# FFN up product with the tokens stationary, its output turned by 32x32 VectorE transposes and a trip through DRAM

## The chip, the core and the metric

One core of a Trainium2 chip runs the whole program: TensorE (PE; its weight loads are shown apart as PEld), VectorE (DVE), ScalarE (ACT), GpSimd (POOL, hardly used here) and SyncE (SP, which issues every DMA of this kernel). The metric is the device time of one execution in microseconds (us).

## What is computed

A decoder trunk of two layers over 256 tokens with 2048 features, in float32. Each layer has a mixer, a cross-attention into 256 memory tokens and a gated feed-forward part (FFN) with a short convolution over the tokens. The change concerns the FFN alone:

```python
def conv_ffn(h, w_up, conv_w, conv_b, w_down):     # h 256 x 2048, w_up 2048 x 11264
    u = causal_dwconv(h @ w_up, conv_w) + conv_b   # 3 taps over tokens, per feature
    g, val = jnp.split(u, 2, axis=-1)
    return (jax.nn.silu(g) * val) @ w_down         # w_down 5632 x 2048
```

`h` is normalised first; the factor of each token (one over its root mean square) is multiplied in after `h @ w_up`, before the convolution.

## The kernel before

Activations lie with features on the 128 partitions and the 256 tokens along the free axis. To keep precision, each operand is split in two float32r parts, high and low, and a product is three partial products: high·high, high·low, low·high. An activation operand `x` has, for each 128 features, 512 columns: 256 tokens high, then 256 low.

`stream` brings in weights: SP loads 1024 columns (512 KB, a **weight tile** in what follows) into `raw` (4 buffers), ACT casts them to `wh`, DVE subtracts to get `wl` (3 buffers of each). Two products use it:

- `wstat` keeps weights stationary. For each 128 input features (a k step; there are 16) and each 128 output features it loads `wh` and streams all 512 columns of `x`, then loads `wl` and streams the 256 high columns. The result has features on partitions, with high and low halves side by side; `fold` adds the halves (ACT copies one out, DVE adds).
- `xstat` keeps tokens stationary. For each k step and each 128 tokens it does three matmuls, each of which streams 512 weight columns: `xh` with `wh`, `xh` with `wl`, `xl` with `wh`. The result has tokens on partitions and 512 features along the free axis. The value projections (`vp`) and the queries of the windowed attention (`zq`) use it.

The FFN up product (`ffn_up`) runs 44 calls of `wstat` per layer, each of 256 features: 128 gate features and the 128 values that they multiply. `ffn_tile` follows each: `fold`, `by_row` (the token factors `rbc`, on DVE), the three taps (one ACT activation with bias, two DVE multiply-adds over shifted tokens, for each of the two halves), Silu on ACT, the product, and `split` into the high and low parts of the operand `a` of the down product.

Engines run their instructions in order. A scheduler at build time sets that order; casts, subtractions and the first reads of a result have priority. Functions that the change touches, with the lines of the profile:

Of the kernel before, what the change touches and what calls it, by code (L numbers as in the profile page):

```python
# [9 lines left out]
F32 = mybir.dt.float32  # L10
# [4 lines left out]
ALU = mybir.AluOpType  # L15
AX = mybir.AxisListType

P = 128
# [5 lines left out]
FT = D_FF // P  # L24
# [22 lines left out]
WPRIO = 100  # L47
# [17 lines left out]
class Task:  # L65


    def __init__(self, gen, after):
        self.gen, self.after, self.wait, self.done = gen, after, 0, False


class Trunk:
    def __init__(self, ctx, tc, a):
        self.tc, self.nc, self.a = tc, tc.nc, a
        pool = lambda name, bufs, **kw: ctx.enter_context(tc.tile_pool(name=name, bufs=bufs, **kw))
        self.const = pool("const", 1)
        self.par = pool("par", 1)
        self.actp = pool("actp", 29)
        self.raw = pool("raw", 4)
        self.wp = pool("wp", 3)  # L80
        self.tmp = pool("tmp", 6)
        self.ev = pool("ev", 3)
        self.col = pool("col", 3)
        self.rb = pool("rb", 2)
        self.pmm = pool("pmm", 2, space=bass.MemoryType.PSUM)
        self.psm = pool("psm", 4, space=bass.MemoryType.PSUM)

        self.tasks = deque()
# [105 lines left out]
    def xstat_both(self, xs, wd, name="mm"):  # L194

        nc = self.nc
        ps = [self.pmm.tile([P, 2, 512], F32, tag="mm", name=name)]
        side = [self.bank(name) for _ in range(2)]
        out = [[ps[0][:, tb, :TOKC] for tb in range(2)], [b[:, :TOKC] for b in side]]
        for k, wh, wl in self.stream(wd, 2 * TOKC, KT):  # L200
            x = xs(k // 2) if callable(xs) else xs[k // 2]
            for tb in range(2):
                xh, xl = (x[:, k % 2, u, tb * P:(tb + 1) * P] for u in range(2))
                for lhs, w, i in ((xh, wh, 0), (xh, wl, 1), (xl, wh, 2)):
                    for c in range(2):
                        nc.tensor.matmul(out[c][tb], lhsT=lhs, rhs=w[:, c * TOKC:(c + 1) * TOKC],  # L206
                                         start=(k == 0 and i == 0), stop=(k == KT - 1 and i == 2))
                self.pump()
        return out


    def fold(self, ps, name="z", z=None):
# [685 lines left out]
        return out, ts  # L898


    def ffn_tile(self, ps, j, rbc, x):
        nc = self.nc
        z = self.fold(ps)
        self.by_row(z, rbc)
        u = self.t512("u", (P, 2, T))
        for s in range(2):
            m = 2 * j + s
            tap = [self.p[:, C_FW + m * 3 + i:C_FW + m * 3 + i + 1] for i in range(3)]
            nc.scalar.activation(u[:, s, :], z[:, s, :], AF.Identity, bias=self.p[:, C_FB + m:C_FB + m + 1], scale=tap[2])  # L909
            nc.vector.scalar_tensor_tensor(u[:, s, 1:T], z[:, s, 0:T - 1], tap[1], u[:, s, 1:T], ALU.mult, ALU.add)  # L910
            nc.vector.scalar_tensor_tensor(u[:, s, 2:T], z[:, s, 0:T - 2], tap[0], u[:, s, 2:T], ALU.mult, ALU.add)
        nc.scalar.activation(u[:, 0, :], u[:, 0, :], AF.Silu)
        nc.vector.tensor_tensor(u[:, 1, :], u[:, 0, :], u[:, 1, :], ALU.mult)
        self.split(x[:, j % 2, 0, :], x[:, j % 2, 1, :], u[:, 1, :])

    def ffn_up(self, l, xs, acc):
        out, wait = [], []
        _, rbc, rt = self.row_factor(acc, "rx", W["ss"])
        for j in range(FT):
            wait.append((self.wstat(xs, self.a["wu"][l, j], name="up"), j))  # L920
            if j == 0:
                continue
            self.until(rt)
            for ps, i in wait:
                if i % 2 == 0:
                    out.append(self.operand(f"a{i // 2}"))
                self.ffn_tile(ps, i, rbc, out[-1])
            wait = []
        return out

    def run(self):
# [23 lines left out]
def _groups(w, gc):  # L955

    d, k, n = w.shape
    w = w.reshape(d, k // P, P, n // gc, gc).transpose(0, 3, 2, 1, 4)
    return np.ascontiguousarray(w).reshape(d, n // gc, P, (k // P) * gc)


def _fm(x):

    return np.ascontiguousarray(x.T.reshape(8, 2, P, T).transpose(0, 2, 1, 3))


def _colmajor(v):

    return np.swapaxes(v.reshape(v.shape[:-1] + (-1, P)), -1, -2)


def _layout(inp):
    sizes = (256, 256, 512, 512, 16, 1024, 128, 128, 512, 512, 512)
    off = np.concatenate([[0], np.cumsum(sizes)])
    gq, gk, gv, gr, lr, sq, sk, sv, cb, cc, ch = (np.arange(off[i], off[i + 1]) for i in range(11))
    heads = sq.reshape(2, 8, 64).transpose(1, 0, 2).reshape(-1)
    fm = [gk, gq, gr]
    for j in range(4):
        fm += [cc[j * P:(j + 1) * P], ch[j * P:(j + 1) * P]]
    w_in = inp["w_in"]  # L980
    d = {}
    d["w_tok"] = _groups(w_in[:, :, np.concatenate([lr, sk, sv, gv])], 2 * TOKC)[:, 0]
    d["w_fm"] = _groups(w_in[:, :, np.concatenate(fm + [cb])], 2 * P)
    d["w_q"] = _groups(w_in[:, :, heads], 512)
    ro = np.arange(2048)
    rows = np.concatenate([ro[1536:], ro[:512],
                           512 + np.arange(1024).reshape(2, 8, 64).transpose(1, 0, 2).reshape(-1)])
    d["wo"] = _groups(inp["w_out"][:, rows, :], 256)
    for n, m in (("wq", "xa_wq"), ("wk", "xa_wk"), ("wxo", "xa_wo"), ("wd", "ffn_w_down")):
        d[n] = _groups(inp[m], 256)  # L990
    d["wd7"] = _groups(inp["ffn_w_down"][-1:, :, 14 * P:], P)[0]
    d["wv"] = _groups(inp["xa_wv"], 512)
    pair = np.arange(2 * D_FF).reshape(2, FT, P).transpose(1, 0, 2).reshape(-1)
    d["wu"] = _groups(inp["ffn_w_up"][:, :, pair], 256)
    d["x"], d["mem"] = _fm(inp["x"][0]), _fm(inp["mem"][0])
    d["mem"] = d["mem"].reshape(4, 2, P, 2, T).transpose(0, 2, 1, 3, 4)
    d["xt"] = inp["x"][0].reshape(2, P, D)
    d["memt"] = inp["mem"][0].reshape(2, P, D)
    d["gmix0"] = _colmajor(inp["norm_mix"][0])
    d["pos"] = inp["positions"].reshape(2, P).T  # L1000
    d["wgate"] = inp["gla_w_gate"]
    d["sinks"] = inp["swa_sinks"]
    d["gfin"] = _colmajor(inp["norm_final"])
    par = np.zeros((DEPTH, P, NPAR), np.float32)
    for c, n in ((C_MIX, "norm_mix"), (C_X, "norm_x"), (C_MEM, "norm_mem"), (C_FFN, "norm_ffn")):
        par[:, :, c:c + 16] = _colmajor(inp[n])
    par[:, :, C_GB:C_GB + 2] = _colmajor(inp["gla_b_gate"])
    par[:, :, C_GN] = inp["gla_norm"]
    par[:, :, C_SC:C_SC + 12] = _colmajor(inp["sc_conv"]).transpose(0, 2, 3, 1).reshape(DEPTH, P, 12)
    fc = inp["ffn_conv"][:, :, pair]  # L1010
    par[:, :, C_FW:C_FW + 264] = _colmajor(fc).transpose(0, 2, 3, 1).reshape(DEPTH, P, 264)
    par[:, :, C_FB:C_FB + 88] = _colmajor(inp["ffn_conv_b"][:, pair])
    d["par"] = par
    con = np.zeros((P, NCON), np.float32)
    con[:, Q_ID:Q_ID + P] = np.eye(P)
    rel = np.arange(P)[:, None] + P - np.arange(T)[None, :]
    con[:, Q_MASK:Q_MASK + T] = np.where((rel >= 0) & (rel < P), 0.0, -1e30)
    con[:, Q_INV:Q_INV + 32] = np.array(ROPE_INV, np.float32)
    d["con"] = con
    s, t = np.arange(P)[:, None] % 64, np.arange(64)  # L1020
    lev = []
    for n in LEVELS:
        tn = t[t % n >= n // 2][None, :]
        lev.append((s // n == tn // n) & (s % n < n // 2))
    lev.append(s == t[None, :])
    d["lev"] = np.concatenate(lev, axis=1).astype(np.int32)
    return {n: np.ascontiguousarray(v) for n, v in d.items()}
# [18 lines left out]
```

## Time and profile before

| | |
|---|---|
| time, median of 3 runs | 2925.98 us (2925.84 to 2926.13) |
| the profiled execution | 2925.97 us, of it 2923.8 us span on the core |
| PE, PEld busy | 2903.3 us (99%), 2524.3 us (86%) |
| DVE, ACT busy | 1926.9 us (66%), 1506.3 us (52%) |
| DMA | 532.41 MB, mean 182 GB/s |
| granted TensorE clock | 1.00 in the FFN up stages |

A matmul's shown duration runs from its entry to its modelled end and overlaps the next one's; the distance between the starts of neighbours tells what one costs. DMAs show the time from issue to landing.

### The profile page before, as it was taken

How to read it: one execution, taken by the hardware profiler on the slowest of the kernel's cores; microseconds unless marked ns; L12 is line 12 of the kernel's file. 1: busy time of each engine (PE TensorE's matmuls, PEld its weight loads, DVE VectorE, ACT ScalarE, POOL GpSimd, SP SyncE). 2: the span in 40 equal slices, each digit the busy share in tenths (PEclk: the TensorE clock that was granted, in tenths of full speed). 3: DMA queues.
4: the chain of work that ended last, by engine and by line, in shares of the span. 5: the costliest groups of instructions: out<-in, count | busy, mean ns of one | idle time of the engine just before them, and what ended most of it. 6: DMA issues, size and time to landing. Idle time of an engine off the chain costs nothing.

```text
span 2923.8 us, 42872 instructions
## 1 busy us (share of the span) xinstructions
PE 2903.3 (99%) x16718; PEld 2524.3 (86%) x16718; DVE 1926.9 (66%) x2867; ACT 1506.3 (52%) x2125; POOL 8.0 (0%) x38
## 2 busy tenths in 40 slices
PE   9999999999999999999999999999999999999998
PEld 8888888888888888888888888888888888888887
DVE  6786665556777777655567766655577777776454
ACT  6565444444555555544455654444455555554443
POOL 0000000000000000000000000000000000000000
PEclk9999999999999999999999999999999999999999
DMA  7556655555565656666664566555556565656664
GB/s 241 157 179 200 189 184 166 173 168 185 185 188 184 190 183 189 190 188 188 183 183 139 168 194 188 185 163 169 173 183 188 184 188 186 188 187 188 188 188 144
DMA packets 149164, 532.41 MB, mean 182 GB/s; under 512 B 17216, under 2 KB 17760, under 8 KB 148960
## 3 DMA queue, kind: packets, MB, share of 16 engines
q1 hardware_dynamic: 148960, 529.66, 59.0%
q8 instruction: 131, 2.15, 0.3%
q14 instruction: 73, 0.60, 0.1%
HBM read 527.50 MB, written 2.10 MB: 181 GB/s over the span
## 4 chain that ended last, share of the span: by engine, by line
PE 98%; DVE 1%; ACT 0%; DMA 0%; issue 0%; SPq 0%; DVEq 0%
PE up L171 21%; PE res L171 19%; PE up L172 11%; PE res L172 9%; PE kp L171 4%; PE qp L171 4%; PE vp L189 2%; PE vp L190 2%; PE vp L188 2%; PE kp L172 2%; PE qp L172 2%; PE tokp L206 2%; PE zc L171 2%; PE up L175 1%; PE zq L190 1%; PE zq L188 1%
## 5 line engine op out<-in xcount | busy, mean ns | idle before, releaser
L156 DVE TENSOR_TENSOR wl<-raw,wh 128x1024 fp32r<-128x1024 f32 (+2 forms) x993 | 1204.2, 1213 | 721.1 <-ACT wh L155 719.2
L155 ACT CAST wh<-raw 128x1024 fp32r<-128x1024 f32 (+2 forms) x993 | 1033.2, 1041 | 939.5 <-PE res L171 303.2
L171 PE MATMUL up<-xs,wh 128*128 128x512 f32 x2640 | 935.9, 399 | 0.0
L172 PE MATMUL up<-xs,wl 128*128 128x256 f32 x2640 | 742.3, 281 | 0.0
L171 PEld LDWEIGHTS up<-xs,wh 128*128 128x128 f32 x2640 | 496.4, 188 | 117.8
L172 PEld LDWEIGHTS up<-xs,wl 128*128 128x128 f32 x2640 | 499.6, 189 | 3.5
L171 PE MATMUL res<-a,wh 128*128 128x512 f32 x1376 | 482.6, 395 | 0.0
L172 PE MATMUL res<-a,wl 128*128 128x256 f32 x1376 | 386.1, 281 | 0.0
L171 PEld LDWEIGHTS res<-a,wh 128*128 128x128 f32 x1376 | 258.1, 188 | 59.8
L172 PEld LDWEIGHTS res<-a,wl 128*128 128x128 f32 x1376 | 260.5, 189 | 0.8
L171 PE MATMUL qp<-xs,wh 128*128 128x512 f32 x480 | 171.2, 397 | 0.0
L171 PE MATMUL res<-xo,wh 128*128 128x512 f32 x480 | 170.5, 399 | 0.0
L171 PE MATMUL kp<-ms,wh 128*128 128x512 f32 x480 | 169.5, 397 | 0.0
L172 PE MATMUL res<-xo,wl 128*128 128x256 f32 x480 | 134.9, 281 | 0.0
L172 PE MATMUL qp<-xs,wl 128*128 128x256 f32 x480 | 134.9, 281 | 0.0
L219 ACT COPY z_b<-up 128x512 f32<-128x512 f32 x88 | 51.6, 587 | 161.3 <-PE up L175 161.3
L172 PE MATMUL kp<-ms,wl 128*128 128x256 f32 x480 | 134.7, 281 | 0.0
L220 DVE TENSOR_TENSOR z<-up,z_b 128x512 f32<-128x512 f32 x88 | 60.8, 691 | 105.7 <-ACT z_b L219 105.7
L909 ACT ACTIVATE u<-z,par 128x256 f32<-128x256 f32 x176 | 96.6, 595 | 48.5 <-DVE z L224 48.5
L171 PEld LDWEIGHTS res<-xo,wh 128*128 128x128 f32 x480 | 90.3, 188 | 21.2
L171 PEld LDWEIGHTS kp<-ms,wh 128*128 128x128 f32 x480 | 90.2, 188 | 21.1
L171 PEld LDWEIGHTS qp<-xs,wh 128*128 128x128 f32 x480 | 90.2, 188 | 18.8
(317 smaller groups left out, 4078.4 us busy)
## 6 DMA issues: line engine op xcount, KB each, us to landing
raw<-in_wu SPq DMA_DIRECT2D x352, 512.0 KB, 4.4
raw<-in_wd SPq DMA_DIRECT2D x175, 512.0 KB, 3.6
raw<-in_w_fm SPq DMA_DIRECT2D x80, 512.0 KB, 4.4
raw<-in_wk SPq DMA_DIRECT2D x64, 512.0 KB, 4.8
raw<-in_wo SPq DMA_DIRECT2D x64, 512.0 KB, 4.5
raw<-in_wq SPq DMA_DIRECT2D x64, 512.0 KB, 3.9
raw<-in_wv SPq DMA_DIRECT2D x64, 512.0 KB, 3.7
raw<-in_wxo SPq DMA_DIRECT2D x64, 512.0 KB, 4.3
```

The source lines that it names most:

```text
L155: nc.scalar.copy(wh[:, :n], raw[:, :n])
L156: nc.vector.tensor_tensor(wl[:, :n], raw[:, :n], wh.bitcast(F32)[:, :n], ALU.subtract)
L171: nc.tensor.matmul(ps[:, m, :], lhsT=wh[:, ms], rhs=xhl, start=(k == 0), stop=False)
L172: nc.tensor.matmul(ps[:, m, 0:T], lhsT=wl[:, ms], rhs=xh, start=False, stop=False)
L175: nc.tensor.matmul(ps[:, m, :], lhsT=wh[:, ms], rhs=xhl, start=False, stop=True)
L188: nc.tensor.matmul(ps[:, tb, :gc], lhsT=xh, rhs=wh, start=(k == 0), stop=False)
L189: nc.tensor.matmul(ps[:, tb, :gc], lhsT=xh, rhs=wl, start=False, stop=False)
L190: nc.tensor.matmul(ps[:, tb, :gc], lhsT=xl, rhs=wh, start=False, stop=(k == KT - 1))
L206: nc.tensor.matmul(out[c][tb], lhsT=lhs, rhs=w[:, c * TOKC:(c + 1) * TOKC], start=(k == 0 and i == 0), stop=(k == KT - 1 and i == 2))
L219: nc.scalar.copy(b, ps[:, :, T:2 * T])
L220: nc.vector.tensor_tensor(z, ps[:, :, 0:T], b, ALU.add)
L909: nc.scalar.activation(u[:, s, :], z[:, s, :], AF.Identity, bias=self.p[:, C_FB + m:C_FB + m + 1], scale=tap[2])
```

## The change

The up product goes through `xstat`: 22 calls per layer, each of 512 features (two gate/value pairs), with the weights laid out by the host in groups of 512 columns. The result has tokens on partitions and must be turned. `turn` does this in two steps. Two DVE transposes (one for each 128 tokens) read PSUM and turn every 32x32 block within its own 32 partitions, into `zt` (`z_t` in the rows). Then a DMA writes `zt` (512 KB) to a DRAM tile `zd` (`z_d`), and four DMAs read it back, each for 32 partitions, into `zf` (shown as `z`), so that the blocks come to the right partitions. Two DVE multiplications put in the token factors, in place of `by_row`, and write the result over `zt`. `fold` is gone here. The taps and what follows are as before. A constructor argument of the program (`dynamic_dma_scratch_size=1024`) gives back memory for the new buffers.

```diff
+        self.turnp = pool("turnp", 2)
+        self.dram = pool("dram", 4, space=bass.MemoryType.DRAM)
...
+    def turn(self, ps, name="z"):
+        nc = self.nc
+        zt = self.turnp.tile([P, 4, 2, 4, 32], F32, tag="zt", name=name + "_t")
+        zf = self.turnp.tile([P, 4, 2, 4, 32], F32, tag="zf", name=name)
+        zd = self.dram.tile([4, 32, 4, 256], F32, tag="zd", name=name + "_d")
+        with self.tc.high_priority(offset=WPRIO):
+            for tb in range(2):
+                nc.vector.transpose(out=zt[:, :, tb].rearrange("p b k i -> p k b i"),
+                                    in_=ps[:, tb, :].rearrange("p (k b i) -> p k b i", k=4, b=4))
+            nc.sync.dma_start(zd.rearrange("a p b f -> (a p) (b f)"), zt.rearrange("p b t k i -> p (b t k i)"))
+            for b in range(4):
+                nc.sync.dma_start(zf[32 * b:32 * b + 32].rearrange("p a t k i -> p a (t k i)"),
+                                  zd[:, :, b, :].rearrange("a p f -> p a f"))
+        return zf, zt.rearrange("p b t k i -> p (b t k i)").rearrange("p (k t) -> p k t", k=4)
...
-    def ffn_tile(self, ps, j, rbc, x):
-        z = self.fold(ps)
-        self.by_row(z, rbc)
+    def ffn_tile(self, z, j, x):
...
     def ffn_up(self, l, xs, acc):
...
-        for j in range(FT):
-            wait.append((self.wstat(xs, self.a["wu"][l, j], name="up"), j))
+        for j in range(0, FT, 2):
+            zf, z = self.turn(self.xstat(xs, self.a["wu"][l, j // 2], name="up"))
...
+            for tb in range(2):
+                ts = slice(tb * P, (tb + 1) * P)
+                nc.vector.tensor_tensor(z[:, :, ts].rearrange("p k (a i) -> p k a i", a=4),
+                                        zf[:, :, tb].rearrange("p a k i -> p k a i"),
+                                        rbc[:, ts].rearrange("p (a i) -> p a i", a=4).unsqueeze(1)
+                                        .broadcast_to([P, 4, 4, 32]), ALU.mult)
+            out.append(self.operand(f"a{j // 2}"))
+            for i in range(2):
+                self.ffn_tile(z[:, 2 * i:2 * i + 2], j + i, out[-1])
...
-    d["wu"] = _groups(inp["ffn_w_up"][:, :, pair], 256)
+    d["wu"] = _groups(inp["ffn_w_up"][:, :, pair], 512)
```

On SP, at the start of an FFN up stage, the kernel before issues nothing but weight loads (176 of `wu` for the layer):

```order
L153 DMA raw<-in_wxo 128x1024 x32
L153 DMA raw<-in_wu 128x1024 x176
L153 DMA raw<-in_wd 128x1024 x6
```

The changed kernel issues there, for each block of 512 features (8 weight tiles), one write and four reads more:

```order
L155 DMA raw<-in_wxo 128x1024 x32
L155 DMA raw<-in_wu 128x1024 x14
L225 DMA z_d<-z_t 128x1024
L155 DMA raw<-in_wu 128x1024
L227 DMA z<-z_d 32x4x256 x4
L155 DMA raw<-in_wu 128x1024 x7
```

The first block's write stands behind 14 weight loads: the 8 of its own block and tiles 0 to 5 of the next one. Its reads stand behind tile 6.

On DVE, in the middle of the stage, the kernel before has these rows from one `wl` to the next `fold` (a half of 512 features):

```order
L156 TENSOR_TENSOR wl<-raw,wh 128x1024
L220 TENSOR_TENSOR z<-up,z_b 128x512
L224 TENSOR_TENSOR z<-z,rxb 128x512
L156 TENSOR_TENSOR wl<-raw,wh 128x1024
L910 SCALAR_TENSOR_TENSOR u<-z,par,u 128x255 x2
L911 SCALAR_TENSOR_TENSOR u<-z,par,u 128x254 x2
...
L913 TENSOR_TENSOR u<-u 128x256
...
L228 TENSOR_TENSOR a_7249<-u,a_7249 128x256
```

The changed kernel has these rows on DVE for a whole block, from the transposes of a block (when PE has ended it) on; between rows that are left out with "..." there is one `wl` row each time:

```order
L223 STREAM_TRANSPOSE z_t<-up 128x4x4x32 x2
L158 TENSOR_TENSOR wl<-raw,wh 128x1024 x3
L944 TENSOR_TENSOR z_t<-z,rxb 128x4x128 x2
L158 TENSOR_TENSOR wl<-raw,wh 128x1024
L928 SCALAR_TENSOR_TENSOR u<-z_t,par,u 128x255 x3
L929 SCALAR_TENSOR_TENSOR u<-z_t,par,u 128x254
L928 SCALAR_TENSOR_TENSOR u<-z_t,par,u 128x255
L929 SCALAR_TENSOR_TENSOR u<-z_t,par,u 128x254 x2
L158 TENSOR_TENSOR wl<-raw,wh 128x1024
L929 SCALAR_TENSOR_TENSOR u<-z_t,par,u 128x254
L931 TENSOR_TENSOR u<-u 128x256
...
```

The `wl` of tiles 0 and 1 of the next block stand ahead of the transposes, those of tiles 2, 3 and 4 between them and the multiplications (L944), which wait for the four reads; tile 5 follows, then seven of the eight tap instructions, then tile 6.

## Rows read from the trace of the kernel before

**Rows 1.** Busy time by engine, and the chain that ended last, shares by engine.

```profile
PE 2903.3 (99%) x16718; PEld 2524.3 (86%) x16718; DVE 1926.9 (66%) x2867; ACT 1506.3 (52%) x2125; POOL 8.0 (0%) x38
...
PE 98%; DVE 1%; ACT 0%; DMA 0%; issue 0%; SPq 0%; DVEq 0%
```

**Rows 2.** The first FFN up stage: us, busy time (instructions), granted clock, DMA share, GB/s.

```profile
715.60:1213.50 497.90, 497.90 (x2826) 432.63 (x2825) 368.60 (x538) 281.80 (x396) 0.00 (x0) 1.00 0.60 186
```

**Rows 3.** Matmuls with `wh` of that stage (as many with `wl`): count, ns minimum/median/maximum, first and last start.

```profile
L171 PE MATMUL up<-xs,wh x1320: 386/398/479, 715.6 to 1212.4; 128*128 128x512 f32 x189
...
L175 PE MATMUL up<-xs,wh x88: 391/394/401, 726.7 to 1213.2; 128*128 128x512 f32 x88
```

**Rows 4.** Its first matmul and the one after its last: start, us, instruction.

```profile
715.62 0.39 PE L171 MATMUL up<-xs,wh 128*128 128x512 f32 x1
...
1213.46 0.39 PE L171 MATMUL res<-a,wh 128*128 128x512 f32 x1
```

**Rows 5.** Value projection by `xstat`: the ends of an uninterrupted run of 30.

```profile
535.18 0.39 PE L189 MATMUL vp<-wl,ms 128*128 128x512 f32 x1
...
541.98 0.39 PE L189 MATMUL vp<-wl,ms 128*128 128x512 f32 x1
```

**Rows 6.** Queries by `xstat`: the ends of a run of 14 behind other matmuls.

```profile
1560.78 0.40 PE L188 MATMUL zq<-wh,xs 128*128 128x512 f32 x1
...
1564.01 0.39 PE L190 MATMUL zq<-wh,xs 128*128 128x512 f32 x1
```

**Rows 7.** DVE and ACT, 800 to 1200 us: count, busy us, mean ns, idle before.

```profile
L156 DVE TENSOR_TENSOR wl<-raw,wh 128x1024 fp32r<-128x1024 f32 x142 | 173.4, 1221 | 58.3 <-ACT wh L155 58.3
L155 ACT CAST wh<-raw 128x1024 fp32r<-128x1024 f32 x142 | 148.6, 1047 | 76.8 <-PE up L171 76.8
...
L220 DVE TENSOR_TENSOR z<-up,z_b 128x512 f32<-128x512 f32 x35 | 24.2, 692 | 44.1 <-ACT z_b L219 44.1
L224 DVE TENSOR_TENSOR z<-z,rxb 128x512 f32<-128x512 f32 x35 | 24.2, 691 | 1.2
L219 ACT COPY z_b<-up 128x512 f32<-128x512 f32 x35 | 20.5, 587 | 66.4 <-PE up L175 66.4
```

**Rows 8.** DVE in order of time, in the first up stage.

```profile
808.82 1.22 DVE L156 TENSOR_TENSOR wl<-raw,wh 128x1024 fp32r<-128x1024 f32 x1
809.95 0.87 DVE L910 SCALAR_TENSOR_TENSOR u<-z,par,u 128x255 f32<-128x255 f32 x2
810.74 0.87 DVE L911 SCALAR_TENSOR_TENSOR u<-z,par,u 128x254 f32<-128x254 f32 x2
...
812.66 0.42 DVE L913 TENSOR_TENSOR u<-u 128x256 f32<-128x256 f32 x1
...
819.51 0.69 DVE L224 TENSOR_TENSOR z<-z,rxb 128x512 f32<-128x512 f32 x1
820.12 1.22 DVE L156 TENSOR_TENSOR wl<-raw,wh 128x1024 fp32r<-128x1024 f32 x1
```

**Rows 9.** DMA issues 801 to 860 us, and the first output write: count, size, issue to landing.

```profile
raw<-in_wu SPq DMA_DIRECT2D x22, 512.0 KB, 4.5
...
out<-h SPq DMA_DIRECT2D x1, 256.0 KB, 2.1
```

**Rows 10.** A DMA issued at 1213.43 us between weight loads, and the very first DMA.

```profile
lr<-in_wgate SPq DMA_DIRECT2D x1, 16.0 KB, 4.3
...
gmix<-in_gmix SPq DMA_DIRECT2D x1, 8.0 KB, 1.6
```

**Rows 11.** Weight loads of the down product, two sizes, whole span.

```profile
raw<-in_wd SPq DMA_DIRECT2D x175, 512.0 KB, 3.6
...
raw<-in_wd SPq DMA_DIRECT2D x2, 256.0 KB, 2.7
```

**Rows 12.** SP's issues at the start: start, us, DMA.

```profile
0.74 0.39 SPq L315 DMA_DIRECT2D gmix<-in_gmix  x1
1.19 0.42 SPq L153 DMA_DIRECT2D raw<-in_w_tok  x1
```

More of the change, by code (lines that the diff above doesn't have):

```diff
@@ L916, in ffn_up @@
     def ffn_up(self, l, xs, acc):
-        out, wait = [], []
+        nc = self.nc
+        out = []
         _, rbc, rt = self.row_factor(acc, "rx", W["ss"])
-        for j in range(FT):
-            wait.append((self.wstat(xs, self.a["wu"][l, j], name="up"), j))
+        for j in range(0, FT, 2):
+            zf, z = self.turn(self.xstat(xs, self.a["wu"][l, j // 2], name="up"))
             if j == 0:
[L922 to L928, printed above, removed]
+                self.until(rt)
+            for tb in range(2):
[7 more added lines that the diff above has]
+                self.ffn_tile(z[:, 2 * i:2 * i + 2], j + i, out[-1])
         return out
@@ L1034 @@
     arrays = _layout({n: np.asarray(v) for n, v in inputs.items()})
-    nc = bacc.Bacc("TRN2", target_bir_lowering=False, num_devices=1)
+    nc = bacc.Bacc("TRN2", target_bir_lowering=False, num_devices=1, dynamic_dma_scratch_size=1024)
     feeds, aps = {}, {}
```

## The prediction

> **What bounds the kernel now.** I read the page's busy shares and chain first, then the stretch of the stage that changes. PE is busy 99% of the span and 98% of the chain [rows 1]; in the FFN up stage it has no idle time at all (497.90 of 497.90 us at granted clock 1.00), while DVE is busy 74%, ACT 57% and the DMA engines 60% [rows 2]. So the stage lasts as long as PE's stream of matmuls, and only two things can move the time: what that stream costs, and whether anything makes PE wait for weights.
>
> What one matmul costs is not its shown duration, since neighbours overlap, but the distance between starts. The first stage has 1320 + 88 matmuls with `wh` and as many with `wl`, so 1408 pairs [rows 3], and lasts from 715.62 to 1213.46 us [rows 4]: 497.84 / 1408 = 353.6 ns a pair of 512 + 256 columns. The second layer's stage is alike.
>
> **The matmuls.** For one k step and 512 features the old form needs 4 pairs, 4 x 353.6 = 1414 ns. The new one needs 6 matmuls of 512 columns (two token blocks by three partial products). The trace has that form already, in the value projection: 30 distances in a row take 541.98 - 535.18 = 6.80 us, 226.7 ns each [rows 5]. 6 x 226.7 = 1360 ns. The columns streamed are equal (4 x 768 = 6 x 512 = 3072); what goes is a quarter of the instructions and of the weight loads. The saving is 54.3 ns a unit; there are 16 k steps x 22 blocks x 2 layers = 704 units: **-38.2 us**. Behind an interruption the same form runs for a while at (1564.01 - 1560.78) / 14 = 230.7 ns [rows 6]; were all of the stage like that, 1384 ns a unit and -21 us. The up stage has next to no other matmuls to interrupt it, so I take 226.7.
>
> At this place the Trainium skill speaks against the change: "TensorE: Matmul & The Clock Gate", section Back-to-back issue gap, puts an isolated matmul of N columns at N / 2.4 + 2.5 ns, so time follows columns. By it a pair costs 325 ns, a unit 1300 before and 1295 after, and the saving is an estimated 4 us. The trace does not agree: 353.6 ns against 325, and 226.7 against 215.8.
>
> **The turn, and who waits for it.** A block now takes 96 x 226.7 ns = 21.76 us of PE, a weight tile an eighth, 2.72 us. Per block of 512 features, `fold`'s two DVE additions (0.692) and two `by_row` (0.691) go [rows 7]; two transposes and two multiplications come. All read or write the same 512 columns, the transposes from PSUM as the addition did. No row shows a transpose. Below, 0.61 us, the pace of one instruction of that size to the next (820.12 - 819.51) [rows 8]; above, twice 0.69 if a block is filled and drained without overlap, 1.4. I take 0.69, because it moves as many elements in and out as the addition. ACT loses its two copies of 0.587 [rows 7]. Two instructions of one kind pass in 0.79 us (810.74 - 809.95), a `wl` in 1.13 (809.95 - 808.82) [rows 8]. DVE's work per block is then 8 x 1.13 + 2 x 0.65 + 2 x 0.65 + 8 x 0.395 + 4 x 0.42 = 16.5 us of 21.76. DVE has enough time; what counts is its order.
>
> DVE works in order, and the multiplications wait for the round trip through DRAM at the head of its queue. Behind them stand the `wl` that PE needs next. Let the block end on PE at 0. Transposes until 1.4 us. SP has then passed tile 5's load and stands at the write. A write of 256 KB lands after 2.1 us [rows 9]; a load of 512 KB takes 0.9 us longer than one of 256 [rows 11], so 3.0 us alone, and at most the 4.5 us of weight loads in this stream [rows 9], since a tile's load is under way ahead of it. I take 4.0: landed at 5.4. The four reads are issued 0.45 us apart (1.19 - 0.74) [rows 12], the last 1.4 us after the first. Its landing takes 1.6 us on an empty queue, 4.3 among weight loads [rows 10]; tile 6's load, issued at about 2.6, is nearly through by then, so I take 2.4. The data are there at Z = 1.4 + 4.0 + 1.4 + 2.4 = **9.2 us**; the bounds are 1.4 + 3.0 + 1.4 + 1.6 = 7.4 and 1.4 + 4.5 + 1.4 + 4.3 = 11.6.
>
> Which of the `wl` behind is late first? From Z on: two multiplications 1.3, tile 5's `wl` 1.13, seven tap instructions 2.75, tile 6's `wl` 1.22: done at Z + 6.4. PE begins tile 6 at 6 x 2.72 = 16.3 and its second matmul, the first that needs `wl`, at 16.55. So DVE may wait until **Z = 10.15** before PE stops; tile 5 (needed at 13.8, done at Z + 2.4) would bear more. At Z = 9.2 the wait of DVE is hidden, with 0.95 us to spare. Each microsecond beyond 10.15 comes back once in a block, 44 times: PE stops, the next block ends later, and so on.
>
> ACT's casts are further from their limit: tile 6's cast (1.047, [rows 7]) stands behind four activations that follow the multiplications, and ends near Z + 4.5, ahead of DVE.
>
> SP's own queue: behind the write waits tile 6's load, behind the reads tile 7's. The latter is issued at 5.4 + 1.8 = 7.2 instead of about 5.1 (when tile 3's `wl` frees its buffer), lands within 4.5 us at 11.7, and PE wants the tile at 19.0: hidden by 7 us. The DMA engines carry 8 x 512 KB plus twice 512 KB per 21.76 us, so 241 GB/s in place of 186; by the same cost per byte that is 60% x 241 / 186 = 78% of them. The reads move 1 KB pieces and may cost more; there is room for it. At the end of each stage the last block's turn runs beside the down product, whose PE needs that operand last in its first sweep over 44 k steps, some 30 us later at 2 pairs a step.
>
> Sum, against the profiled execution's 2925.97 us (which is the median of 2925.98): -38.2, and nothing for the turn: **2888 us**.
>
> **Rivals.**
>
> *The round trip is late (slower).* The mechanism is the one above with Z past 10.15: multiplications hold DVE, tile 6's `wl` comes late, PE stops once in every block. It cancels the saving at 10.15 + 38.2 / 44 = 11.0 us, and decides from there. At the upper bound, Z = 11.6, it costs 1.45 x 44 = 64 us: 2926 - 38 + 64 = 2952. Transposes of 1.4 us alone put Z at 10.6: +20, 2908; together with the upper bound Z = 13.0 and 3013. For it speaks that two dependent DMAs stand in a row and share the engines with the weights; against it, that the nearest write takes 2.1 us, half of what I allow. Chance of ending slower 0.25; of a partial loss that still leaves it faster, 0.12.
>
> The Trainium skill's "DMA: Bandwidth & Descriptors", section Anatomy of one DMA — SWDGE (gpsimd) path, says that the receipt of a write is slowest into HBM. Here the trace has an HBM write of 256 KB at 2.1 us beside loads of that size at 2.7.
>
> *Columns alone set PE's time.* If a unit costs what its 3072 columns cost in the old form (353.6 / 768 = 0.460 ns a column), 1414 ns stay 1414 and the time is 2926. Against it: 226.7 / 512 = 0.443 ns a column in rows of this trace, in a stage with the same casts and subtractions beside it. Chance 0.06. (The formula of the Trainium skill's page "TensorE: Matmul & The Clock Gate", section Back-to-back issue gap, would come out here, 4 us below 2926.)
>
> *The slower spacing*, 230.7 ns all along, as queues behind DVE's transposes or PSUM reads might make it: 2905. Chance 0.10, within "faster".
>
> **Numbers.** The likeliest case, all of the gain, has 0.47, partial loss 0.12, slower spacing 0.10: faster 0.69. Columns alone 0.06, which with a wait that just cancels the gain makes "within 0.2%" 0.06; slower 0.25. A measurement of this kernel can tell about 0.2% (6 us) from no change. The likeliest case's own range is 2884 to 2894: 4 us below for a spacing 1 ns shorter than any row shows, 6 above for short stops. The range that holds 8 in 10 reaches down to 2884 and up to the round trip's upper bound, 2952; slower transposes together with a slow round trip are left out.
>
> **What would show it.** The matmuls `up<-wh,xs` at 226 to 228 ns from start to start, 2112 in a stage, and stages of 479 us. PE without idle time in them. The transposes near 0.7 us. DVE waiting for the four reads at L944 for 1 to 2 us a block, with the reads landing 8 to 10 us after the block's last matmul. If I am wrong, PE's idle time stands ahead of tile 6 in each block, released by `wl`, and the reads' landing or the transposes say which; or the spacing is over 230 ns with PE never idle.

## The result and the profile after

The changed kernel takes 2948.58 us (2948.32 to 2948.97, 4 runs) against 2926.06 us beside it: ratio 1.0077, 95% interval 1.0063 to 1.0091, so 22.5 us slower where 38 us faster had been forecast. What came true is the rival of the late round trip, which the prediction had given 0.25.

The page after, with busy time by engine and the shares of the chain that ended last [rows 1]:

```profile
PE 2884.8 (98%) x15310; PEld 2445.7 (83%) x15310; DVE 1914.7 (65%) x2867; ACT 1460.6 (50%) x2037; POOL 8.0 (0%) x38
...
PE 73%; DMA 12%; DVE 10%; issue 3%; SPq 2%; ACT 0%; DVEq 0%
```

TensorE's share of the chain falls from 98 to 73%, and the transfers of the turn stand in it. Both FFN up stages, in windows from their first matmul to their last (us, then busy time by engine, granted clock, DMA share, GB/s) [rows 2]:

```profile
715.00:1223.10 508.10, 489.09 (x2121) 394.80 (x2121) 359.29 (x530) 257.59 (x349) 0.00 (x0) 1.00 0.70 225
2174.20:2683.70 509.50, 489.11 (x2123) 394.89 (x2122) 359.35 (x530) 257.60 (x349) 0.00 (x0) 1.00 0.70 224
```

A stage lasts 508 to 510 us instead of 498, and TensorE, which had no idle time there, now shows 19 to 20 us of it in each (less than the stops cost, as shown below); the two stages account for 10.2 + 11.6 = 21.8 of the 22.3 us by which the span grew. The tile `up` tells what the matmuls, the transposes and the waits for them are (ns minimum/median/maximum; idle time in us, times) [rows 3]:

```profile
L190 PE MATMUL up<-wh,xs x1408: 387/389/476, 715.0 to 2683.0; 128*128 128x512 f32 x176
...
L191 PE MATMUL up<-wl,xs x1408: 387/389/504, 715.3 to 2683.2; 128*128 128x512 f32 x176
...
L223 DVE STREAM_TRANSPOSE z_t<-up x88: 673/696/718, 738.0 to 2684.5; 128x512 f32<-128x512 f32 x88
...
  DVE wl L158: 104.3, 117
```

The transposes are as priced, 0.696 us. It is `wl` that TensorE waits for, and the waits of the whole span say why (who waits for whom: us in all, times, longest):

```profile
DVE z_t L944 <- DMA z<-z_d: 150.7, 44, 5.0
...
PEld up L191 <- DVE wl L158: 64.9, 63, 1.9
```

By the starts of the matmuls, TensorE stops ahead of tile 6's second matmul in 41 of the 42 blocks that follow another one in their stage (0.7 to 1.3 us from start to start), and in 15 of them ahead of tile 5's as well (0.39 to 1.86 us). VectorE stands at the multiplications (L944) in every one of the 44 blocks, 3.4 us on average, where 1 to 2 us had been forecast. The chain that ended last, in order of time, through one block of the first stage (start, us, what):

```profile
805.39 0.24 PE up L192
805.70 0.60 issue
806.30 0.69 DVE z_t L223
807.00 4.70 DMA z_d<-z_t
811.72 0.33 SPq L227
812.04 0.06 issue
812.10 0.75 SPq L227
812.89 0.43 SPq L227
813.36 3.92 DMA z<-z_d
817.41 0.10 DVE z_t L944
817.50 0.51 issue
818.02 0.68 DVE z_t L944
818.70 1.14 DVE wl L158
819.84 1.19 DVE u L928 x3
...
822.52 1.23 DVE wl L158
823.79 0.50 PE up L191
```

This is the first rival link by link: the block's last matmul, transposes, write (4.70 us), four issues, the last read (3.92 us), then behind the multiplications tile 5's `wl`, taps, tile 6's `wl`, and only then TensorE's matmul with tile 6's `wl` at 823.79. This trip, 11.8 us, is so long that TensorE stops for tile 5's `wl` too, which ends at 819.84. Its timeline there (idle time before an instruction in brackets):

```profile
819.06 0.39 PE L190 MATMUL up<-wh,xs 128*128 128x512 f32 x1
819.89 0.50 PE L191 MATMUL up<-wl,xs 128*128 128x512 f32 x1 [0.45 <-DVE wl L158]
820.23 0.39 PE L192 MATMUL up<-wh,xs 128*128 128x512 f32 x1
```

0.83 us pass between the first two starts where 0.227 would do. The bracket says 0.45 because the first matmul's shown duration runs on; distances between starts are again the measure. (The prediction let tile 5 bear a trip of 13.8 - 2.4 = 11.4 us; this one is longer.)

### The profile page after: what moved, and what is told of

Read it like the earlier page. It is cut to its first block, busy times and chain, and to the rows that moved or that the text cites. A ratio compares the mean times of both kernels' runs of the same rounds, so it can differ in the third digit from the quotient of the medians.

```text
span 2946.1 us, 40277 instructions
## 1 busy us (share of the span) xinstructions
PE 2884.8 (98%) x15310; PEld 2445.7 (83%) x15310; DVE 1914.7 (65%) x2867; ACT 1460.6 (50%) x2037; POOL 8.0 (0%) x38
## 4 chain that ended last, share of the span: by engine, by line
PE 73%; DMA 12%; DVE 10%; issue 3%; SPq 2%; ACT 0%; DVEq 0%
PE res L173 18%; PE res L174 9%; DMA z_d<-z_t 7%; DMA z<-z_d 5%; PE kp L173 4%; PE qp L173 4%; PE up L191 4%; DVE wl L158 4%; PE up L192 3%; PE up L190 3%; DVE u L928 2%; PE vp L192 2%; PE vp L190 2%; PE vp L191 2%; PE qp L174 2%
## 5 line engine op out<-in xcount | busy, mean ns | idle before, releaser
L191 PE MATMUL up<-wl,xs 128*128 128x512 f32 x1408 | 555.4, 394 | 39.4 <-DVE wl L158 39.4
L192 PE MATMUL up<-wh,xs 128*128 128x512 f32 x1408 | 548.9, 390 | 0.0
L190 PE MATMUL up<-wh,xs 128*128 128x512 f32 x1408 | 548.5, 390 | 0.0
L191 PEld LDWEIGHTS up<-wl,xs 128*128 128x128 f32 x1408 | 264.1, 188 | 118.7 <-DVE wl L158 64.9
L190 PEld LDWEIGHTS up<-wh,xs 128*128 128x128 f32 x1408 | 264.3, 188 | 55.8
L192 PEld LDWEIGHTS up<-wh,xs 128*128 128x128 f32 x1408 | 264.4, 188 | 53.0
L927 ACT ACTIVATE u<-z_t,par 128x256 f32<-128x256 f32 x176 | 91.6, 591 | 144.7 <-DVE z_t L944 144.7
L944 DVE TENSOR_TENSOR z_t<-z,rxb 128x512 f32<-128x512 f32 x88 | 56.9, 689 | 150.7 <-DMA z<-z_d 150.7
```

The source lines that it names most:

```text
L190: nc.tensor.matmul(ps[:, tb, :gc], lhsT=xh, rhs=wh, start=(k == 0), stop=False)
L191: nc.tensor.matmul(ps[:, tb, :gc], lhsT=xh, rhs=wl, start=False, stop=False)
L192: nc.tensor.matmul(ps[:, tb, :gc], lhsT=xl, rhs=wh, start=False, stop=(k == KT - 1))
L944: nc.vector.tensor_tensor(z[:, :, ts].rearrange("p k (a i) -> p k a i", a=4), zf[:, :, tb].rearrange("p a k i -> p k a i"), rbc[:, ts].rea ...
```

## The experiments

**First round: is it the order on VectorE, the traffic, or the matmuls?** Theory A: the round trip's end holds VectorE at the head of its queue, and with it the `wl` behind. Theory B: the traffic, or SyncE standing still for the write, holds up the weight loads. Theory C: the matmul form or the transposes cost more than thought.

*late6* holds back the multiplications and what follows them on VectorE until a later `wl` has been issued; no data, buffer or DMA changes:

```diff
-            zf, z = self.turn(self.xstat(xs, self.a["wu"][l, j // 2], name="up"))
...
+            first = len(self.wls)              # wls: every wl subtraction, in order
+            ps = self.xstat(xs, self.a["wu"][l, j // 2], name="up")
+            if held:
+                with self.tc.issue_after(self.wls[first + 6].ins):
+                    finish(*held)              # multiplications and ffn_tile of the block before
+            held = (*self.turn(ps), j)
```

> Only the order on VectorE changes: the two multiplications of a block, which wait for the four reads, stand behind the subtraction (wl) of tile 6 of the next block instead of tile 4; all DMAs stay. Theory A (the trip's end, 11.1 us after the block, holds VectorE at the head of its queue and so delays the wl of tile 6): tile 6's wl is no longer behind the wait, TensorE does not stop, stages of 479 to 481 us, 2888 to 2893 us. Theory B (the trip's traffic, and SyncE's queue that stands still for the write, hold up the weight loads themselves): about 2948 us as before, with casts waiting for loads.

Measured: 2892.24 us (ratio 0.9885, 0.9871 to 0.9900), within A's numbers.

*lateT* goes further: the multiplications of a block are issued behind the transposes of the next one.

```diff
+            zf, z, turned = self.turn(ps)      # turned: the second transpose
+            if held:
+                with self.tc.issue_after(turned.ins):
+                    finish(*held)
```

> The multiplications of a block are issued on VectorE only behind the transposes of the next block, a whole block (21.8 us) later, so no trip of 11 to 13 us can hold VectorE; all DMAs stay. Theory A: VectorE never waits for the reads, 2888 to 2895 us. Theory B: about 2948 us.

Measured: 2889.61 us (0.9877, 0.9860 to 0.9893), 59 us below the changed kernel and 36.5 below the kernel before, the fastest version that leaves nothing out. Its stages (windows as above) have no idle time on TensorE, though the DMA engines carry the same turn at a higher rate. They are 28 to 30 us shorter than the changed kernel's, and that is what the stops cost there:

```profile
714.90:1194.60 479.70, 479.70 (x2121) 397.42 (x2120) 355.66 (x516) 254.36 (x341) 0.00 (x0) 1.00 0.76 239
2145.10:2624.90 479.80, 479.80 (x2123) 397.46 (x2122) 355.76 (x516) 254.32 (x341) 0.00 (x0) 1.00 0.76 239
```

and VectorE passes from transposes to multiplications without a wait, since what they need landed 12 us earlier (the write of this turn was issued at 804.49, and its trip of 11.1 us ended at 814.04):

```profile
824.91 1.31 DVE L224 STREAM_TRANSPOSE z_t<-up 128x512 f32<-128x512 f32 x2 [0.41 <-PE up L193]
826.15 1.25 DVE L942 TENSOR_TENSOR z_t<-z,rxb 128x512 f32<-128x512 f32 x2
827.32 1.22 DVE L159 TENSOR_TENSOR wl<-raw,wh 128x1024 fp32r<-128x1024 f32 x1
```

*notrip* leaves out the write and the reads; the transposes write `zf` and the multiplications read it:

```diff
-            nc.sync.dma_start(zd.rearrange("a p b f -> (a p) (b f)"), zt.rearrange("p b t k i -> p (b t k i)"))
-            for b in range(4):
-                nc.sync.dma_start(zf[32 * b:32 * b + 32].rearrange("p a t k i -> p a (t k i)"),
-                                  zd[:, :, b, :].rearrange("a p f -> p a f"))
```

> The write and the four reads are left out (the output is not the reference's: blocks of 32 are turned, but not moved between partitions); matmuls, transposes and multiplications stay. Theories A and B: 2887 to 2891 us, 226.7 ns from matmul to matmul, no idle time on TensorE in the stage. Theory C (the matmul form or the transposes themselves cost more than the rows of before said): over 2900 us.

Measured: 2889.24 us (one run). C falls: the new form with its transposes, without the trip, is worth 2926.16 - 2889.24 = 36.9 us. And B has nothing left: *lateT* with all the traffic is 0.4 us from *notrip* with none.

*far* makes the trip longer by a copy within DRAM:

```diff
+            ze = self.dram.tile([4, 32, 4, 256], F32, tag="ze", name=name + "_e")
+            nc.sync.dma_start(ze.rearrange("a p b f -> (a p) (b f)"), zd.rearrange("a p b f -> (a p) (b f)"))
```

> A second hop: between write and reads a copy of 512 KB from DRAM to DRAM, so the trip gets longer by one DMA of 4 to 5 us and the reads land near 16 us after the block. The multiplications now stand behind tile 5's wl, so VectorE may wait 2.7 us longer than in the changed kernel, until about 12.7 us. Theory A: TensorE stops for some 3.3 us a block, 44 x 3.3 = 145 us, 3030 us (each us of the trip beyond the limit comes back 44 times). Theory B: no such law; the extra 23 MB of traffic alone would cost a few us, 2950 to 2975 us.

Measured: 3070.05 us (one run). The trip ends 16.5 us after the block on average (16 expected), and the multiplications wait longer (us, times, longest):

```profile
DVE z_t L946 <- DMA z<-z_e: 235.6, 40, 7.6
```

The direction is A's, the time is 40 us above its number. Two things make up 36 of them: the trip was 0.46 us longer than expected, 44 x 0.46 = 20 us, and a block that stopped lasted 9.42 us more than the trip where the expected limit of 12.7 would have meant 21.76 - 12.7 = 9.06, 44 x 0.36 = 16 us. Most of the second is a lower clock (last section).

**Second round: what makes the trip so long, and is there a remedy without an order by hand?**

*quiet* issues the load of tile 6 behind the reads, on SyncE alone:

```diff
-                nc.sync.dma_start(raw[:, :n], wd[:, k * gc:k * gc + n])
+                behind = self.read if k // kp == 6 else None       # the last of the four reads
+                with self.tc.issue_after(behind) if behind else nullcontext():
+                    nc.sync.dma_start(raw[:, :n], wd[:, k * gc:k * gc + n])
```

> Only SyncE's order changes: the load of tile 6 of the next block is issued behind the four reads instead of between write and reads, so the reads share the DMA engines with no weight load that was issued after the write; VectorE's order is that of the changed kernel (multiplications behind tile 4). Theory A1 (the reads are late because they share the rings with weight loads): the last read lands about 2.4 us after its issue as the prediction had it, the trip ends near 9.9 us, at VectorE's limit, 2890 to 2905 us. Theory A2 (a write and four reads of 1 KB pieces take that long by themselves): the trip still ends at 10.8 to 11.3 us, 2935 to 2950 us.

Measured: 2932.51 us (1.0026, 1.0015 to 1.0037), the trip 10.98 us. The runs lie between 2931.47 and 2938.36 us, and the profiled one, which the trip is from, is the longest; the time is the median. Moving the load takes a quarter of a microsecond off the trip of that execution; A1 falls, at least for loads issued between write and reads.

*flat* reads in one piece:

```diff
-            for b in range(4):
-                nc.sync.dma_start(zf[32 * b:32 * b + 32].rearrange("p a t k i -> p a (t k i)"),
-                                  zd[:, :, b, :].rearrange("a p f -> p a f"))
+            nc.sync.dma_start(zf.rearrange("p a t k i -> p (a t k i)"), zd.rearrange("a p b f -> (a p) (b f)"))
```

> One read of 512 KB in rows of 4 KB takes the place of the four reads of 1 KB pieces (the output is not the reference's: blocks stay on their partitions). Theory A1: a weight-sized read among weight loads lands 4.7 us after its issue, the trip ends at 6.3 + 4.7 = 11.0 us as before, about 2945 us. Theory A2 (the four issues and the small pieces are what costs): the read lands after 3.5 us as an undisturbed load, the trip ends at 9.8 us, 2890 to 2900 us.

Measured: 2919.68 us (one run), the trip 10.6 us, its read landing after 4.3 us on average. Between the two expectations: one read of the whole costs less than four issues and a last read, but only by 0.6 us.

*wp4* gives the weights a fourth buffer:

```diff
-        self.raw = pool("raw", 4)
-        self.wp = pool("wp", 3)
+        self.raw = pool("raw", 3)
+        self.wp = pool("wp", 4)
...
-        zf = self.turnp.tile([P, 4, 2, 4, 32], F32, tag="zf", name=name)
+        zf = self.turnp.tile([P, 4, 2, 4, 32], F32, tag="zf", name=name, bufs=1)
```

> Four buffers of wh and wl instead of three (three of raw instead of four and one zf instead of two to make room). The wl run one tile further ahead, and the multiplications stand behind tile 5's wl instead of tile 4's. Theory A: VectorE's limit moves by a tile, from 9.9 to about 12.6 us, past nearly all trips of 10 to 12.8 us; TensorE stops rarely, 2889 to 2896 us, without any change of order by hand. Rival (three raw buffers starve the casts): over 2910 us, with casts waiting for loads.

Measured: 2987.57 us (1.0211, 1.0196 to 1.0226): slower still, and the rival named with it is right. Its waits:

```profile
ACT wh L157 <- DMA raw<-in_wu: 265.6, 182, 3.2
...
DVE z_t L944 <- DMA z<-z_d: 178.2, 44, 5.4
```

With three raw buffers the casts wait for loads. The transposes stand behind a further `wl`, tile 2's, that has to be made first, so they begin 3.2 us after the block's end (median) instead of 0.2, and the trip ends at 14.6. The edit changes three pools at once; a fourth `wh` and `wl` with four raw buffers was not tried.

*gpread* issues the reads from another engine:

```diff
-                nc.sync.dma_start(zf[32 * b:32 * b + 32].rearrange("p a t k i -> p a (t k i)"),
+                nc.gpsimd.dma_start(zf[32 * b:32 * b + 32].rearrange("p a t k i -> p a (t k i)"),
```

> The four reads are issued by GpSimd instead of SyncE; SyncE no longer stands still for the write. The multiplications stand behind tile 5's wl here, so the limit is about 12.6 us. Theory A: only the end of the trip counts; if GpSimd's reads end the trip at 11 to 12.5 us, 2889 to 2900 us; if at 14 us, 44 x 1.4 = 62 us more, 2950 us. Theory B (SyncE's standing still was what hurt) would give 2889 us whatever the reads' landing.

Measured: 3047.78 us (one run). SyncE no longer waits for the write, yet the time is 99 us above the changed kernel's: B falls a second time. The trip ends at 16.1 us, later than the 11 to 14 that A had named; by the limit that the table below gives, 21.76 - 9.36 = 12.4, A's reckoning would be 2889 + 44 x 3.66 = 3050 us. A read issued by GpSimd lands after 5.9 us (median, by the DMA issues of this kernel: count, size, us) instead of 3.0:

```profile
z<-z_d POOLq DMA_DIRECT2D x176, 128.0 KB, 5.9
```

**Third round: the law from the other side, and the reads by themselves.** From the starts of the matmuls and the landings, each run gives 44 trips (from 227 ns after the start of the block's last matmul to the landing of its last read) and 42 distances from block end to block end within a stage. Trips and blocks are those of the profiled execution, times are medians; they are of executions within 3 us of each other, except in *quiet*, whose profiled execution took 2938.36 us:

| run | multiplications behind | trip, mean us | block, mean us | block minus trip, where TensorE stopped | time, us |
|---|---|---|---|---|---|
| changed kernel | tile 4 | 11.21 | 23.14 | 11.91 (42 blocks) | 2948.58 |
| quiet | tile 4 | 10.98 | 22.90 | 11.90 (38) | 2932.51 |
| alone | tile 4 | 10.73 | 22.66 | 11.91 (39) | 2929.13 |
| flat | tile 4 | 10.57 | 22.49 | 11.85 (26) | 2919.68 |
| wp4 | tile 5 | 14.61 | 23.93 | 9.20 (39) | 2987.57 |
| gpread | tile 5 | 16.06 | 25.41 | 9.36 (42) | 3047.78 |
| far | tile 5 | 16.46 | 25.89 | 9.42 (42) | 3070.05 |
| late5 | tile 5 | 11.37 | 21.78 | 9.16 (3) | 2893.25 |
| late6 | tile 6 | 11.61 | 21.77 | one block, at its first matmul | 2892.24 |
| lateT | next block | 10.95 | 21.76 | never | 2889.61 |

*late5* is *late6* with `first + 5`:

> All DMAs and buffers as in the changed kernel; on VectorE the multiplications stand one wl further back, behind tile 5's instead of tile 4's. In the runs so far a block that stopped TensorE lasted the trip's length plus 11.9 us with the multiplications behind tile 4, and plus 9.2 to 9.4 us behind tile 5. By that law a block of 21.76 us allows a trip of 12.4 us here; of the changed kernel's trips (mean 11.2, longest 12.85) only a few are longer: 2889 to 2893 us. Rival (the position does not matter by itself, the other runs differ in more than that): between 2900 and 2950 us.

Measured: 2893.25 us (0.9890, 0.9874 to 0.9907), with three stopped blocks. One `wl` further back is worth 55 us.

*alone* makes tile 6's load wait for the four reads to land:

```diff
-                nc.sync.dma_start(raw[:, :n], wd[:, k * gc:k * gc + n])
+                behind = self.read if k // kp == 6 else None       # the four reads
+                load = nc.sync.dma_start(raw[:, :n], wd[:, k * gc:k * gc + n])
+                for read in behind or ():
+                    self.tc.add_manual_dep(load.ins, read.name, mybir.DependencyInfo(
+                        mybir.DependencyClass.Sync, mybir.DependencyReason.DATA), reason="alone")
```

> As the run in which tile 6's load follows the reads, and that load also waits until all four reads have landed, so that nothing of SyncE's stands beside the reads. If the reads' landing 3.4 us after the last issue (2.4 in the prediction) came from loads issued behind them, it falls to 2.4 to 2.7 us and the trip to 10.0 us; if reads of this form take that long by themselves, it stays at 3.2 to 3.5 us and the trip at 10.8. The time says less here: tile 6's load now comes late and may stop TensorE by itself: 2900 to 2990 us.

Measured: 2929.13 us (one run). The last read lands 3.12 us after its issue (3.48 in the changed kernel, 3.35 in *quiet*), nearer to "by themselves". Loads behind the reads explain 0.36 us of the 1.1 that the forecast missed there.

## Why the prediction was wrong, by its own steps

**The matmuls: right.** 226.7 ns from start to start was read from the value projection, and the median distance in the new stage is 227 ns; the form with its transposes gave 36.9 of the forecast 38.2 us (*notrip*). "Columns alone" is refuted.

**The transposes, DVE's work, the cover of the weight loads, the end of the stage: right.** 0.696 us for 0.69; stages of 479.7 us in *lateT*, which has all of that work in them; casts there wait for a weight load once in the first stage, 1.6 us in all.

**The order on VectorE and the law: right.** The limit was worked out at 10.15 us. A block lasts the trip plus 11.91 us, so TensorE begins to stop at 21.76 - 11.91 = 9.85 us, 0.3 earlier, which is 44 x 0.3 = 13 us of the loss. The sentence that each microsecond beyond comes back once in a block holds: in the changed kernel's own 42 blocks the trips run from 10.1 to 12.9 us, and block minus trip stays between 11.80 and 12.06. One tile further back shifts the limit by 11.91 - 9.16 = 2.75 us (*late5*, which changes the order alone), a tile's 2.72.

**The trip, Z = 9.2 us: the step that failed.** The mechanism was right, its size was not: the mean is 11.21 us, past the limit, within bounds of 7.4 to 11.6. Of the 2.0 us that are missing, the write is 0.77, the last read 1.08, and the start and the first issue 0.16.

The write lands after 4.77 us on average, not 4.0, and so even beyond its own bound of 4.5. The 2.1 us on which the prediction leaned [rows 9] are of a write with no weight load beside it: the DMA engines' share was 0.01 in the 15 us before. Among loads, the prediction reckoned with one weight tile under way. That is so in the first block of each stage only, where the write takes 3.4 and 3.3 us and the trip 10.1 and 10.6. In the other 42 blocks two or three loads are under way when the write is issued, and it takes 4.84 us. The wait itself brings them together. Behind it VectorE makes the late `wl` one soon after the other; each frees a buffer and lets SyncE issue a load that waited for it, and the last two loads go out 3.3 and 1.7 us ahead of the write. In *lateT* the `wl` come evenly, the loads go out 4.4 and 1.7 us ahead, one is under way in 37 of 44 blocks, and the write takes the 4.0 us of the forecast. The last two `wl` ahead of the transposes in the chain above, and in *lateT*:

```profile
802.49 1.22 DVE L158 TENSOR_TENSOR wl<-raw,wh 128x1024 fp32r<-128x1024 f32 x1
...
804.07 1.23 DVE L158 TENSOR_TENSOR wl<-raw,wh 128x1024 fp32r<-128x1024 f32 x1
```

```profile
820.60 1.23 DVE L159 TENSOR_TENSOR wl<-raw,wh 128x1024 fp32r<-128x1024 f32 x1 [1.50 <-ACT wh L158]
823.28 1.23 DVE L159 TENSOR_TENSOR wl<-raw,wh 128x1024 fp32r<-128x1024 f32 x1 [1.45 <-ACT wh L158]
```

No run changes the number of loads alone, so that this is what lengthens the write is read from the traces and not tested.

The last read lands 3.48 us after its issue, not 2.4, and *alone*, with no weight load beside the reads, shows that 3.1 of it is the read's own in this form, close behind three others. The DMA issues of the changed kernel (count, size, median us from issue to landing) [rows 9, 10], and of *lateT*:

```profile
z_d<-z_t SPq DMA_DIRECT2D x44, 512.0 KB, 4.7
z<-z_d SPq DMA_DIRECT2D x176, 128.0 KB, 3.0
```

```profile
z_d<-z_t SPq DMA_DIRECT2D x44, 512.0 KB, 4.0
z<-z_d SPq DMA_DIRECT2D x176, 128.0 KB, 3.7
```

In *lateT* the reads are slower in their turn (the last one lands after 3.98 us, with 3.3 loads beside it on average instead of 2.3), and the trip is 10.95 us: too long for the order of the changed kernel even with the write as forecast.

With 11.21 in the forecast's own formula the time would have been 2926 - 38 + 44 x (11.21 - 10.15) = 2935, so this step alone turns the forecast round; with the measured limit 2926 - 36.9 + 44 x (11.21 - 9.85) = 2949, against 2948.58 measured. That the last figure agrees so closely is in part luck: only 42 of the 44 trips have a further block of their stage behind them. The forecast had a margin of 0.95 us on a sum of four terms with a spread of 4.2 between its bounds, and gave the hidden case 0.47; the middle of those bounds, 9.5, already left only 0.65.

**What stays open.** How a read's own 3.1 us divides between its start, its 1 KB pieces and its landing was not tried apart; *flat* moves piece size, number of issues and size of a transfer together. That two issues in the row of four took 0.75 and 0.43 us instead of 0.33 is in the chain above, and its cause was not tried; the row as a whole took the 1.4 us of the forecast.

## What to carry to other kernels

An engine that works in order turns a hidden latency into a visible one as soon as the instruction that waits stands ahead of work that another engine needs. Work out the deadline of each instruction behind the waiting one; when the margin is smaller than the spread of the latency, price the loss, and put the wait where it has a whole block of slack. Moving the multiplications, and what follows from them, back by one subtraction was worth 55 us here, by a whole block 59. When two dependent DMAs stand in a row beside a stream of loads, take landing times from that stream, not those of an idle queue, and ask whether the wait itself will bunch the stream: what an engine does late it then does in quick succession.

## What the runs showed of the hardware that was not expected

Stops of TensorE can have a second price. In the changed kernel, with 19 us of idle time in a stage, the granted clock stays at 1.00. In *far*, with 58 us of idle time in 566, it is 0.96 on average over the stage, and back at 1.00 behind it:

```profile
715.40:1281.50 566.10, 507.56 (x2122) 408.56 (x2121) 356.14 (x529) 257.85 (x349) 0.00 (x0) 0.96 0.68 221
1282.00:1460.00 178.00, 175.09 (x998) 152.48 (x997) 96.52 (x110) 76.23 (x86) 0.00 (x0) 1.00 0.66 197
```

The average hides short stretches at 0.50, which is 1.2 GHz instead of 2.4, behind the stop at tile 6 in 23 of the 42 blocks. Matmuls start 427 ns apart there instead of 227. One of them (the window, then TensorE's rows in it):

```profile
860.40:863.70 3.30, 2.90 (x7) 2.33 (x8) 3.30 (x9) 2.68 (x6) 0.00 (x0) 0.50 0.51 154
```

```profile
860.80 0.80 PE L191 MATMUL up<-wl,xs 128*128 128x512 f32 x1 [2.74 <-DVE wl L158]
861.39 0.63 PE L192 MATMUL up<-wh,xs 128*128 128x512 f32 x1
861.82 0.63 PE L190 MATMUL up<-wh,xs 128*128 128x512 f32 x1
```

The 23 blocks last the trip plus 9.62 us, the other 19 the trip plus 9.17, like those of *late5* and *wp4* (9.16 and 9.20). In *gpread* (0.98 over the first stage, 0.97 over the second) it is 9.69 us in 19 blocks with such a stretch and 9.09 in the 23 without. So the lower clock is what sets these two runs apart in the table, at about half a microsecond a block that has it. Which stops it follows is open: in *far* it followed some in which two starts were 2.5 us apart and not others of 3.7.

Four reads of 128 KB issued by GpSimd took twice as long to land as those by SyncE, 5.9 against 3.0 us. The number of SyncE's loads beside them does not account for it: three loads on average overlap the last read in *gpread* and in *quiet*, and it lands after 6.2 us in the one and 3.35 in the other. Whether the argument `dynamic_dma_scratch_size=1024` has a part in it was not tried. And a write of 512 KB to DRAM lands after about the time that a weight load of that size takes beside it: 4.7 us against 4.8 in the changed kernel, 4.0 against 4.3 in *lateT* (medians).
